# A two-layer diffusion step: the attention gate's modulation moved to VectorE, the output projection reordered, four weight buffers instead of five

## The chip, the cores and the metric

The kernel runs on one core of one Trainium2 chip. The core has five engines that run side by side and wait for each other through semaphores: TensorE (matmuls), VectorE, ScalarE, GpSimd, and SyncE, which here only issues transfers. The metric is device time in microseconds of one launch. The profile calls the engines PE (PEld is its loading of stationary operands), DVE, ACT, POOL and SP.

## The reference

One inference step of a two-layer network over 128 context tokens and 256 latent tokens, with 1024 features. Layer 0 mixes tokens by attention, layer 1 by a gated MLP; both are followed by a gated feed-forward network with a width-3 convolution. Six modulation vectors per layer come from a conditioning vector, one for context and one for latent tokens.

```python
def adaln(cond, w_ada, b_ada):
    mod = jax.nn.silu(cond) @ w_ada + b_ada
    return jnp.split(mod[:, None, :], 6, axis=-1)      # sm, cm, gm, sf, cf, gf

for l in range(2):
    sm, cm, gm, sf, cf, gf = adaln(c, w_ada[l], b_ada[l])
    h = rmsnorm(x, norm_mix_g[l]) * (1 + cm) + sm
    mix = attention(h) @ w_attn_out if l == 0 else chunk_gmlp(h, ...)
    x = x + gm * mix
    h = rmsnorm(x, norm_ffn_g[l]) * (1 + cf) + sf
    x = x + gf * conv_ffn(h, ...)
```

`w_ada` is 1024 x 6144 for each layer. In attention each latent token attends to 4 rows of 16 neighbours of its 4 x 64 grid with a learned bias, and to 128 cached context keys in the same softmax; context tokens attend to each other. There are 16 heads of 64 features.

## The kernel before

Features lie on the partitions (8 blocks `k` of 128), the 384 tokens on the free axis. Every float32 matmul is done as three: each operand is split into a rounded high half (a cast on ScalarE, line 96 or 108) and the low remainder (a subtraction on VectorE, line 97 or 109), and `mac` (lines 103 to 105) multiplies high by high, high by low and low by high. Weights come in units of 512 KB (128 x 1024): a transfer into one of three staging buffers, the cast into a buffer of the pool `whp`, the subtraction into one of `wlp`. Both pools have five buffers.

The stages follow each other: values of attention, attention by pairs of heads, output projection, feed-forward 0, gated MLP, feed-forward 1, output. From the attention by pairs to the first output tiles the order on TensorE, ScalarE, VectorE and SyncE is the order of the program text, written out by hand (`tc.manual_schedule`). Elsewhere a list scheduler fixes each engine's order before the run, by program order and readiness by its own estimates; `load(src, 50)` gives a unit's two halves 50 places of precedence.

*Modulations.* A part of them is computed on TensorE (class `Ada`): a block of 512 KB (`adw`) holds 128 rows of `w_ada` times one of the six vectors, four matmuls with 32 columns of conditioning run on it (line 190; each shows as two records), and after eight blocks ScalarE copies the sums and TensorE transposes them (`flush`, line 206). Here this is done for the gate GM and for SF and CF of layer 0: 24 blocks, three in each of the eight rounds. The rest is computed on VectorE (class `AdaV`): a transposed block of 512 KB gives one of eight parts of one vector, by one multiply-and-sum reduction (line 248) for each of the two conditionings and a small add (line 250). It needs the conditioning broadcast to all partitions (`cs`, two tiles, activated on ScalarE at line 239), which is prepared after attention. Both classes take their `adw` from one pool of four buffers.

*Rounds.* Round `t` works on a pair of heads. Its queries and keys were made in the round before; it computes scores for two blocks of latent queries, exponentials (line 534), the normalization (lines 539 and 541), and the transposes of the pair before (line 549) with the copies `turned`; between them TensorE has the products of the next pair (`products`, 24 matmuls each) and the values of the pair before (line 566). `ready` casts the next unit and fetches another (line 448). `bias` and `queries` (line 483) stand behind the second `ready`. At a round's end come `ada.run(3)` and `ada.load(3)`, then the next round issues the cached keys (`kT`, one buffer, line 468) on the same queue.

*Output projection.* `output(m, ks)` adds the blocks `ks` of output tile `m` (24 matmuls when complete); `residual` adds the gated tile to `x`, squares it, and `early` writes the next stage's raw input `hhi`, `hlo` of block `m` (line 342). Four tiles are begun before the last pair's values are there, and finished one after another.

*Starts of stages.* `norm_first` lets the next stage start before its RMS norm is known: four units multiply the raw input, and their results are scaled afterwards (`late`). Meanwhile `modulated` (lines 326 to 330) overwrites `hhi` and `hlo` with the normalized input for the units that follow.

## Time and profile before

| | |
|---|---|
| median of 3 runs | 1021.97 us (1020.61 to 1024.64) |
| the profiled execution's own time | 1021.36 us |
| its span (first to last instruction) | 1019.6 us |
| mean granted TensorE clock | 0.993 |
| busy share PE / DVE / ACT / POOL | 98% / 76% / 47% / 1% |

The profile page gives busy times by engine, then the chain of work that ended last, then groups of instructions by line: engine, operation, `out<-in`, shapes, count, busy time, mean duration, and the idle time of the engine just before them with what ended it. A timeline row gives start, duration, engine, line and operation; in brackets stands the idle time before it and its releaser. A row by windows gives, for a stretch of time, the busy time of PE, PEld, DVE, ACT and POOL, then the granted clock, the busy share of the DMA engines and GB/s.

### The profile page before, as it was taken

What the parts mean: (1) busy time and instruction counts of PE and PEld (TensorE: products, weight loads), DVE (VectorE), ACT (ScalarE), POOL (GpSimd) and SP (SyncE); (2) the same over time, 40 slices, a digit from 0 to 9 for tenths busy, and PEclk for the clock granted to TensorE, in tenths of its full rate; (3) what the DMA queues carried; (4) which work ended last, traced back from release to release, by engine and by line L of the source; (5) the groups of instructions that cost most, each with busy time, mean ns of one, the idle gap of its engine ahead of it and who ended that gap; (6) DMA issues with size and microseconds to landing.
All of it is one profiled execution on the core that took longest, in us unless ns stands there. A gap on an engine that the chain in (4) does not pass through costs nothing.

```text
span 1019.6 us, 15979 instructions
## 1 busy us (share of the span) xinstructions
PE 998.2 (98%) x6030; PEld 948.6 (93%) x6030; DVE 775.7 (76%) x1588; ACT 480.6 (47%) x841; POOL 14.7 (1%) x29
## 2 busy tenths in 40 slices
PE   7999999999999999999999999999999999999996
PEld 6788888789999999999998889999999999999996
DVE  3546566577999888999979989888598777777652
ACT  3355556557655555433354434343485444443331
POOL 1000000000000000000000000000000000000000
PEclk8999999999999999999999999999999999999999
DMA  7874645633465545576737746566325434335521
GB/s 277 310 233 143 214 172 201 227 103 126 136 191 169 163 147 161 146 240 205 225 119 257 241 158 200 179 207 186 104 83 166 144 124 125 124 114 171 161 72 62
DMA packets 53932, 172.96 MB, mean 170 GB/s; under 512 B 6224, under 2 KB 12512, under 8 KB 53856
## 3 DMA queue, kind: packets, MB, share of 16 engines
q1 hardware_dynamic: 52992, 170.11, 51.9%
q0 software_dynamic: 432, 1.06, 0.3%
q8 instruction: 47, 0.77, 0.3%
q10 hardware_dynamic: 432, 0.79, 0.2%
q14 instruction: 29, 0.24, 0.1%
HBM read 169.31 MB, written 2.62 MB: 169 GB/s over the span
## 4 chain that ended last, share of the span: by engine, by line
PE 91%; DMA 3%; ACT 2%; DVE 1%; issue 1%; SPq 1%; POOL 0%; POOLq 0%; ACTq 0%
PE bank L103 28%; PE bank L105 28%; PE bank L104 28%; DMA kT<-in_ckT 2%; DMA adw<-in_w_ada 1%; PE bank L781 1%; PE bank L145 1%; PE bank L566 1%; PE bank L517 1%; PE bank L190 1%; PE bank L549 1%; PE bank L282 0%; ACT pr L534 0%; SPq L66 0%; PE bank L300 0%
## 5 line engine op out<-in xcount | busy, mean ns | idle before, releaser
L96 ACT CAST hi<-st 128x1024 fp32r<-128x1024 f32 (+1 forms) x192 | 197.7, 1031 | 302.3 <-PE bank L104 249.0
L105 PE MATMUL bank<-hhi,lo 128*128 128x384 f32 (+1 forms) x960 | 325.1, 339 | 0.2 <-DVE lo L109 0.2
L103 PE MATMUL bank<-hhi,hi 128*128 128x384 f32 (+1 forms) x960 | 325.0, 339 | 0.0
L104 PE MATMUL bank<-hlo,hi 128*128 128x384 f32 (+1 forms) x960 | 324.7, 338 | 0.0
L97 DVE TENSOR_TENSOR lo<-st,hi 128x1024 fp32r<-128x1024 f32 (+1 forms) x192 | 229.9, 1198 | 67.9 <-ACT hi L96 67.6
L105 PEld LDWEIGHTS bank<-hhi,lo 128*128 128x128 f32 x960 | 181.1, 189 | 0.5 <-DVE lo L109 0.5
L103 PEld LDWEIGHTS bank<-hhi,hi 128*128 128x128 f32 x960 | 181.1, 189 | 0.4 <-ACT kT L473 0.2
L104 PEld LDWEIGHTS bank<-hlo,hi 128*128 128x128 f32 x960 | 180.4, 188 | 0.1
L248 DVE CUSTOM_DVE_ANT_0 junk<-adw,cs 128x1024 bf16<-128x1024 f32 x112 | 136.5, 1219 | 1.0
L105 PE MATMUL bank<-ahi,lo 128*128 128x384 f32 x352 | 118.9, 338 | 0.0
L104 PE MATMUL bank<-alo,hi 128*128 128x384 f32 x352 | 118.9, 338 | 0.0
L103 PE MATMUL bank<-ahi,hi 128*128 128x384 f32 x352 | 118.7, 338 | 0.0
L104 PEld LDWEIGHTS bank<-alo,hi 128*128 128x128 f32 x352 | 66.1, 188 | 0.0
L105 PEld LDWEIGHTS bank<-ahi,lo 128*128 128x128 f32 x352 | 66.1, 188 | 0.0
L103 PEld LDWEIGHTS bank<-ahi,hi 128*128 128x128 f32 x352 | 66.1, 188 | 0.0
L103 PE MATMUL bank<-hi,hhi 128*128 128x512 f32 x144 | 57.6, 404 | 1.8 <-ACT hhi L328 1.8
L104 PE MATMUL bank<-lo,hhi 128*128 128x512 f32 x144 | 57.4, 398 | 0.0
L105 PE MATMUL bank<-hi,hlo 128*128 128x512 f32 x144 | 57.3, 399 | 0.0
L374 DVE SCALAR_TENSOR_TENSOR x<-bank,mod,x 128x128 f32<-128x128 f32 x64 | 23.8, 412 | 35.9 <-PE bank L105 35.9
L103 PE MATMUL bank<-mhi,hi 128*128 128x384 f32 x128 | 43.3, 339 | 0.0
L105 PE MATMUL bank<-mhi,lo 128*128 128x384 f32 x128 | 43.2, 338 | 0.0
L104 PE MATMUL bank<-mlo,hi 128*128 128x384 f32 x128 | 43.1, 337 | 0.0
(154 smaller groups left out, 1268.4 us busy)
## 6 DMA issues: line engine op xcount, KB each, us to landing
st<-in_w_up SPq DMA_DIRECT2D x88, 512.0 KB, 3.6
adw<-in_w_adaT SPq DMA_DIRECT2D x56, 512.0 KB, 3.7
adw<-in_w_ada SPq DMA_DIRECT2D x40, 512.0 KB, 5.8
st<-in_w_down SPq DMA_DIRECT2D x32, 512.0 KB, 3.6
st<-in_w_qk SPq DMA_DIRECT2D x16, 512.0 KB, 3.6
st<-in_w_gu SPq DMA_DIRECT2D x16, 512.0 KB, 4.3
st<-in_w_gv SPq DMA_DIRECT2D x16, 512.0 KB, 4.5
st<-in_w_gout SPq DMA_DIRECT2D x16, 512.0 KB, 4.4
```

What stands on the lines that cost most here:

```text
L96: nc.scalar.copy(hi[:, :n], st[:, :n])
L97: nc.vector.tensor_tensor(lo[:, :n], st[:, :n], hi[:, :n].bitcast(F32), ALU.subtract)
L103: nc.tensor.matmul(out, a[0], b[0], start=start, stop=False)
L104: nc.tensor.matmul(out, a[0], b[1], start=False, stop=False)
L105: nc.tensor.matmul(out, a[1], b[0], start=False, stop=stop)
L145: nc.tensor.matmul(pa[32 * j:32 * j + 32, 0:P], cond_s[:, 4 * hf + kk, :], w[hf][:, kk, P * q:P * q + P], start=(kk == 0), stop=(kk == 3), ...
L190: nc.tensor.matmul(self.pa[32 * j:32 * j + 32, 0:256], cond_s[:, k, :], t[:, 256 * j:256 * j + 256], start=(k == 0), stop=(k == KD - 1), t ...
L248: tc.keep_in_program_order(nc.vector.tensor_tensor_reduce(self.junk, t, self.cs[c], 1.0, 0.0, ALU.mult, ALU.add, m[:, c:c + 1]))
L374: nc.vector.scalar_tensor_tensor(x[m][:, a:b], ps[:, a:b], mod(l, gate, m, c), x[m][:, a:b], ALU.mult, ALU.add)
L517: nc.tensor.matmul(sc[hh][:, cols], q[qp][HS[hh], qs:qs + P], k[kp][HS[hh], ks], start=i == 0, stop=i == 2)
L549: nc.tensor.transpose((ta[:, o:o + P] if g < 2 else tb[:, o - 512:o - 512 + P]), pr[:, b, g * P:g * P + P], ident)
L566: nc.tensor.matmul(pv[64 * hh:64 * hh + 64, cols], vv[:, P * t + 64 * hh:P * t + 64 * hh + 64], pT[hh][:, o:o + n], start=start, stop=stop ...
```

## The change

The gate GM of layer 0 leaves `Ada` and heads the list of `AdaV`. Of `AdaV.run`, loading a block and the two reductions become calls of their own (`load`, `half`), so that each round computes one block of the gate: one reduction behind each of its two normalizations. TensorE keeps SF and CF, 16 blocks: two before the first round and two in each of the first seven. `flush` no longer stands at the head of every block but after the queries. The broadcast conditioning is prepared before the rounds, in memory that comes from one buffer fewer in `whp` and in `wlp`.

In the last round there are no modulation matmuls; output tile 0 starts right behind the last scores, ahead of the transposes. Tiles 0 to 2 are begun early instead of 0 to 3, tile 2 lends its blocks 5 and 6 to stand behind the last values, and tiles 3 to 7 run whole, in banks of four pools, the residuals of tiles 0 to 4 three tiles behind. In `norm_first` the four units run one after another over blocks 0 to 6, and then each adds block 7; before, every block ran through all four units.

```diff
-    whp = ctx.enter_context(tc.tile_pool(name="whp", bufs=5))
-    wlp = ctx.enter_context(tc.tile_pool(name="wlp", bufs=5))
+    whp = ctx.enter_context(tc.tile_pool(name="whp", bufs=4))
+    wlp = ctx.enter_context(tc.tile_pool(name="wlp", bufs=4))
...
-            order = [(0, GM), (0, SF), (0, CF)]
+            order = [(0, SF), (0, CF)]
...
         def one(self, l, pc, k, t):
-            self.flush()
...
-            self.todo = (both(1, SM, CM)[:8]
+            self.todo = (one(0, GM) + both(1, SM, CM)[:8]
...
+        def load(self):
+            l, pc, k = self.todo.pop(0)
+            t = adp.tile([P, D], F32, name="adw", tag="adw")
+            nc.sync.dma_start(t, w_adaT[l, pc, k])
+            return l, pc, k, t
+
+        def half(self, c, l, pc, k, t):
+            m = mods[l][:, pc, k]
+            tc.keep_in_program_order(nc.vector.tensor_tensor_reduce(
+                self.junk, t, self.cs[c], 1.0, 0.0, ALU.mult, ALU.add, m[:, c:c + 1]))
+            if c:
+                nc.vector.tensor_scalar(m, m, b_ada[:, l, pc * 8 + k:pc * 8 + k + 1], None, ALU.add)
+                if pc in (CM, CF):
+                    gain(l, pc, slice(k, k + 1))
...
-        for k in range(KD):
+        for ks in (range(KD - 1), (KD - 1,)):
             for wi, p in zip(w, ps):
-                mac(p[:, :NT + 2], wsel(wi, k, slice(0, P)), h(k, slice(0, NT + 2)),
-                    k == 0, k == KD - 1)
+                for k in ks:
+                    mac(p[:, :NT + 2], wsel(wi, k, slice(0, P)), h(k, slice(0, NT + 2)),
+                        k == 0, k == KD - 1)
...
         nc.gpsimd.dma_start(sv_out, V[:, 0, :])
+        ada_v.start(csp)
...
-        ada.load(3)
+        ada.load(2)
+        block = ada_v.load()
...
         Q = queries(p)
+        ada.run(2)
+        ada.load(2)
...
             normalized(*e)
+            ada_v.half(0, *block)
...
-            if last:
-                ada.run(3)
-            else:
+            if not last:
                 K = keys(t + 1, kT, p)
             e = exps(1, sc, pr, pc)
+            if last:
+                break
...
             normalized(*e)
+            ada_v.half(1, *block)
+            p = products()
+            ready()
+            bias(btr)
+            Q = queries(p)
+            ada.flush()
+            if old is not None:
+                values(t - 1, pT)
+            ada.run(2)
+            block = ada_v.load()
+            ada.load(2)
...
         output(0, range(6), ps_mm)
+        pT.append(turned(1, turn(*old[1])))
+        normalized(*e)
         ready()
-        values(6, pT, ps_sc)
+        pv = bank(ps_sc)
         output(1, range(6), ps_sc)
+        values(6, pT, pv)
         ready()
+        ada_v.half(1, *block)
         pT = [turned(0, turn(pr[0], pc[0]))]
+        ada.flush()
         output(0, (6,))
         output(1, (6,))
         pT.append(turned(1, turn(pr[1], pc[1])))
-        output(2, range(7), ps_mm)
-        ready()
+        output(2, range(5), ps_mm)
         values(7, pT)
-        output(3, range(7), ps_sc)
-        ada.flush()
-        for m in range(4):
+        output(2, (5, 6))
+        for m in range(3):
             output(m, (7,))
-            residual(0, GM, m, out[m][1], (0, SF, CF))
-            if m == 1:
+        for m in range(3, KD):
+            output(m, range(KD), (ps_sc, ps_ta, ps_ad, ps_mm, ps_sc)[m - 3])
+            if m < KD - 1:
                 ready()
+            residual(0, GM, m - 3, out[m - 3][1], (0, SF, CF))
         order.__exit__(None, None, None)
-        for m in range(4, KD):
-            output(m, range(KD), ps_mm if m % 2 else ps_sc)
-            if m < KD - 2:
-                ready()
+        for m in range(KD - 3, KD):
             residual(0, GM, m, out[m][1], (0, SF, CF))
...
+    csp = ctx.enter_context(tc.tile_pool(name="cs", bufs=1))
     with tc.tile_pool(name="att", bufs=1) as pool, tc.tile_pool(name="attw", bufs=2) as wkp:
         attention(pool, wkp)
-    csp = ctx.enter_context(tc.tile_pool(name="cs", bufs=1))
-    ada_v.start(csp)
```

## The prediction, made before the changed kernel was seen

> **What bounds the kernel now.** I read the page first: the shares of busy time and the chain that ended last.

> ```profile
> span 1019.6 us, 15979 instructions
> PE 998.2 (98%) x6030; PEld 948.6 (93%) x6030; DVE 775.7 (76%) x1588; ACT 480.6 (47%) x841; POOL 14.7 (1%) x29
> PE 91%; DMA 3%; ACT 2%; DVE 1%; issue 1%; SPq 1%; POOL 0%; POOLq 0%; ACTq 0%
> L96 ACT CAST hi<-st 128x1024 fp32r<-128x1024 f32 (+1 forms) x192 | 197.7, 1031 | 302.3 <-PE bank L104 249.0
> ```

> TensorE is busy for 98% of the span, so outside the places where it waits only removed TensorE work can help, and every new wait costs its full length. The last row says that the casts of weights mostly sit idle until TensorE releases a buffer (249.0 us): they run as far ahead as the buffers let them. I then looked for the stretches in which something else leads, in the timeline of each engine. The first is the loop over the eight head pairs. Here is one round of it, rows picked from the timelines of VectorE, ScalarE, SyncE and TensorE (start, duration, line, tiles, in brackets the idle time before and what ended it), under the group of the six key issues of the full rounds.

> ```profile
> L468 SPq DMA_DIRECT2D kT<-in_ckT x6: 376/408/637, 87.6 to 166.8; - x6
> 119.24 0.42 SPq L468 DMA_DIRECT2D kT<-in_ckT  x1
> 124.27 0.48 DVE L541 TENSOR_SCALAR pc<-pc,st 128x128 f32<-128x128 f32 x2
> 125.20 1.22 DVE L109 TENSOR_TENSOR lo<-st,hi 128x1024 fp32r<-128x1024 f32 x1 [0.45 <-ACT hi L108]
> 127.00 0.62 ACT L108 CAST khi<-kT 128x512 fp32r<-128x512 f32 x1 [1.18 <-DMA kT<-in_ckT]
> 127.66 0.69 DVE L109 TENSOR_TENSOR klo<-kT,khi 128x512 fp32r<-128x512 f32 x1 [1.23 <-ACT khi L108]
> 130.38 0.75 DVE L541 TENSOR_SCALAR pr<-pr,st 128x384 f32<-128x384 f32 x2
> 131.98 1.22 DVE L109 TENSOR_TENSOR lo<-st,hi 128x1024 fp32r<-128x1024 f32 x1 [0.85 <-ACT hi L108]
> 132.63 1.50 PE L190 MATMUL bank<-adw,cond_s 128*32 128x256 f32 x24
> 133.23 0.33 SPq L448 DMA_DIRECT2D st<-in_w_qk  x1
> 133.66 1.33 SPq L176 DMA_DIRECT2D adw<-in_w_ada  x3
> 135.08 0.64 SPq L468 DMA_DIRECT2D kT<-in_ckT  x1
> ```

> The key issues run from 87.6 to 166.8, that is five intervals of 15.84 us, and this round has 135.08 - 119.24 = 15.84. It closes on itself without TensorE: the issue at 119.24 stands on SyncE behind four 512 KB loads, the cast of the keys waits for its landing until 127.00 (7.76 us), keys, exponentials, copies and the cast of the next unit take until 131.98, the second subtraction ("lo") ends at 133.20, its end frees the staging buffer for the fetch at 133.23, three modulation loads follow on the same queue, and then the next key issue. So in the rounds a us off TensorE gains nothing, and a us in this chain costs a us.

> **The added reductions.** Each round gets two VectorE reductions of 1219 ns, the second followed by an add of 221 ns:

> ```profile
> L248 DVE CUSTOM_DVE_ANT_0 junk<-adw,cs 128x1024 bf16<-128x1024 f32 x112 | 136.5, 1219 | 1.0
> L250 DVE TENSOR_SCALAR mod<-mod,b_ada 128x2 f32<-128x2 f32 x56 | 12.4, 221 | 0.4
> ```

> The first stands after 124.27 + 0.48 = 124.75. It fills the wait of 0.45 us, pushes the first "lo" by 0.8 us to 127.2, and the key subtraction at 127.66 still finds the engine free: nothing. The second stands after 130.38 + 0.75 = 131.13 and ends, with the add, near 132.5, where "lo" now starts at 131.98. Behind it wait the fetch, three modulation loads and the keys: 0.5 us in each of the six full rounds, 3.0 us. The queue itself keeps its length, one load for VectorE and two for TensorE instead of three.

> **The removed matmuls and the first round.** Three blocks are 24 records in 1.44 us (132.63 to the next matmul), so 0.48 us a block. In the rounds this is off the chain and counts nothing, likewise the transposes of the gate, now absent. The first round:

> ```profile
> 72.99 0.44 PE L517 MATMUL bank<-khi,qhi 64*128 64x384 f32 x2 [0.58 <-ACT qhi L482]
> 82.74 0.75 DVE L541 TENSOR_SCALAR pr<-pr,st 128x384 f32<-128x384 f32 x2
> 83.48 1.23 DVE L109 TENSOR_TENSOR lo<-st,hi 128x1024 fp32r<-128x1024 f32 x1
> 85.11 2.36 SPq L176 DMA_DIRECT2D adw<-in_w_ada  x3
> ```

> Two blocks (0.96 us) come ahead of the first scores, 0.58 of it in a wait. Their two reloads go out on SyncE ahead of the next keys, some 0.9 us of issue (1.33 / 3 x 2) and 1 MB of traffic; I take 0.8 us for both. Here "lo" follows the normalization at once (82.74 + 0.75 = 83.49), so the second reduction costs 1.3 us. The three loads took 2.36 us at 85.11 against 1.33 later; the earlier release of buffers should save half of that 1.0. So +1.6 us. Rounds together: 1.6 + 3.0 = **+4.5** (bounds 0, if VectorE's place is hidden, and 6).

> **The last round and the output projection.** This is where the change gains:

> ```profile
> 185.14 0.64 PE L190 MATMUL bank<-adw,cond_s 128*32 128x256 f32 x8 [0.77 <-DMA adw<-in_w_ada]
> 186.42 0.64 PE L190 MATMUL bank<-adw,cond_s 128*32 128x256 f32 x8 [0.64 <-DMA adw<-in_w_ada]
> 187.69 0.64 PE L190 MATMUL bank<-adw,cond_s 128*32 128x256 f32 x8 [0.63 <-DMA adw<-in_w_ada]
> 188.26 0.87 PE L549 MATMUL bank<-ident,pr 128*128 128x128 f32 x6
> 186.92 0.48 DVE L541 TENSOR_SCALAR pc<-pc,st 128x128 f32<-128x128 f32 x2
> 187.85 1.23 DVE L109 TENSOR_TENSOR lo<-st,hi 128x1024 fp32r<-128x1024 f32 x1 [0.45 <-ACT hi L108]
> 213.44 0.48 PE L103 MATMUL bank<-ohi,hi 128*128 128x384 f32 x1 [1.86 <-DVE x L374]
> 213.60:217.10 3.50, 3.50 (x12) 3.50 (x12) 2.79 (x7) 3.50 (x7) 0.00 (x0) 0.51 0.00 0
> ```

> The last three blocks wait for their loads one after another: from 185.14 - 0.77 to 188.26 is 3.9 us, all gone. The wait of 1.86 us for the residual that frees a bank goes too: the whole tiles get banks of pools that are idle by then, and a residual has a tile of matmuls beside it. Right behind this wait the granted clock fell.

> In the stretch from 213.60 to 217.10 the clock (the third number from the end) is 0.51, so 3.5 us did the work of 1.8: 1.7 us lost, which I take as gone with the wait. Against it stands 1.0 us: the first reduction of the last round comes between 186.92 + 0.48 and the "lo" at 187.85 and holds it until near 188.55, so it ends near 189.75, while TensorE, with no blocks to wait for, asks for this low half at 184.4 + 18 matmuls of output tile 0 (0.175 us each, from the two last rows of the next fence: 3.2) + the transposes (0.87) + 2 matmuls = 188.8. And 0.3 us for the moved transposes and the last split of the attention output, which now has two blocks of output tile 2 as its cover (6 matmuls, 1.06 us, against a cast and a subtraction of about that length); were that cover missing, it would be 1 us. Sum: -3.9 - 1.9 - 1.7 + 1.0 + 0.3 = **-6.2** (bounds -7.5 and -4).

> [...]

> **The starts of the next three stages.** Each begins with four weight units on the raw input, and only then is the input rewritten, scaled. The last of the three (the others have the same shape):

> ```profile
> 727.66 1.05 ACT L96 CAST hi<-st 128x1024 fp32r<-128x1024 f32 x1 [3.21 <-PE bank L104]
> 728.18 0.42 PE L103 MATMUL bank<-hhi,hi 128*128 128x386 f32 x1
> 728.74 1.23 DVE L97 TENSOR_TENSOR lo<-st,hi 128x1024 fp32r<-128x1024 f32 x1 [0.20 <-ACT hi L96]
> 734.14 1.01 DVE L326 SCALAR_TENSOR_TENSOR t<-x,mod,R 128x128 f32<-128x128 f32 x3 [1.60 <-ACT R L351]
> 736.79 1.00 DVE L326 SCALAR_TENSOR_TENSOR t<-x,mod,R 128x128 f32<-128x128 f32 x3
> 743.03 0.89 DVE L330 SCALAR_TENSOR_TENSOR hlo<-t,mod,hhi 128x128 fp32r<-128x128 f32 x2 [0.43 <-ACT hhi L328]
> 745.46 1.98 ACT L96 CAST hi<-st 128x1024 fp32r<-128x1024 f32 x2
> 746.65 0.34 PE L103 MATMUL bank<-hhi,hi 128*128 128x384 f32 x1
> 747.00 0.33 PE L105 MATMUL bank<-hhi,lo 128*128 128x384 f32 x1
> ```

> The four units take 746.65 - 728.18 = 18.5 us, and the fifth follows without a gap, for two reasons. Its cast (727.66) and its subtraction (728.74) are done before the stage begins, in the fifth buffer; and the rewriting starts at 734.14, because the old order reads block k of all four units before block k + 1, so that the first block is free after an eighth of the stage. It goes at 2.65 us for two blocks (734.14 to 736.79). The change takes both away. With four buffers the fifth unit's cast must wait until the first unit ends, which is where the casts at 745.46 stand; and with unit after unit the old first block is read last when the fourth unit begins: 22 of 32 groups of matmuls, 12.7 us, near 740.9. From there eight low halves and six scalings remain (two can be made ahead): 14 halves of 2.65 / 4, 9.3 us, so the last block is rewritten near 750.7, with 0.5 for the first cast. The fifth unit would use it at 746.65 + 21 matmuls = 750.3.

> Added to that is its own "lo" of 1.2 us, which formerly stood ahead of the stage. If VectorE takes it at once, the rewriting ends near 751.9 and TensorE loses 1.6 us; if it comes behind the rewriting, TensorE stands at its third matmul (747.0) until 751.9 and loses 4.9. A gain is excluded: no wait stands here now. The lower bound is 0, should the next unit's matmuls fill the hole. I take 3, between the two orders, because the engine's queue shows waits of only 0.43 us in which a "lo" can slip in. Three starts: **+9** (0 to 15, and 20 with a fall of the clock behind each stall).

> **Priced at nothing.** Two activations prepare the conditioning:

> ```profile
> L239 ACT ACTIVATE cs<-cs 128x1024 f32<-128x1024 f32 x2 | 2.0, 1050 | 0.0
> ```

> They move ahead of the rounds, where ScalarE (47%) has room; in front of the first casts they could cost their 2 us and a wait for their loads. In the steady parts one unit of run-ahead less (24 matmuls, 4.2 us) still leaves two whole units, some 8 us, since the casts wait for TensorE there (the page's row of 249.0 us); were VectorE late by more than that, its place in the row would turn into TensorE's wait.

> **The sum** stands against the profiled execution's own 1021.4 us (the median of the three runs is 1022.0): 1021.4 + 4.5 - 6.2 + 9 = 1028.7 us.

> **Rivals.** First, the new starts are covered: the order written out in advance fills the hole with the next unit's matmuls and slips the "lo" into the waits of VectorE. For it speaks that TensorE shows no gap there now; against it that VectorE has 9.3 us of work after 740.9 and TensorE 9.4 until 750.3, with the extra "lo" of 1.2 still to come. It decides by whether TensorE's first wait behind a start is under 0.5 us. Then 1028.7 - 9 = 1019.7, not slower. Second, TensorE bounds the rounds after all, and its blocks leave: 0.4 - 7 x 0.48 = -3.0 in place of +4.5, so 1021.2, and with the first rival also true 1012.2. Against it speaks the constant interval of 15.84. Third, the "lo" comes last at all three starts and the clock halves behind each: 14.7 + 5.1 instead of 9, so 1039.5. For it speaks that a wait of 1.86 us was enough for a fall. Fourth, the half clock near the end of attention belongs to no wait and stays: 1028.7 + 1.7 = 1030.4; the row of 0.51 right behind the wait speaks against it. [...]

> **How the numbers follow.** The forecast has 0.33 (its own range is 1024 to 1035), the half clock that stays 0.05, the starts covered 0.22, the rounds bound by TensorE 0.10, both of these 0.13, the serial starts 0.17. A measurement here can tell about 0.5%, 5.1 us, from no change: the marks are 1016.9 and 1027.1. Faster is nearly all the joint case, with a little of the covered one: 0.17. Same holds most of the covered case, the second rival alone and a fifth of the forecast: 0.36. Slower is the rest: 0.47. A range from 1014 to 1039 leaves most of the joint case below it and part of the serial one above.

> **What the profile would show.** Key issues 16.3 us apart instead of 15.84, with "lo" of a round's second half waiting for no cast but starting when VectorE is free; TensorE waiting about 1.5 us a round. No gap near 185 to 188 and none between the output tiles, and a clock of 1.0 where it fell. Behind the fourth unit of each start a wait of TensorE of 1.6 to 4.9 us for "lo" or for the rewritten input. I am wrong if those waits are absent, if the key interval does not grow, or if ScalarE stands in the first 20 us for the conditioning.

## The result and the profile after

The changed kernel takes 1040.13 us (median of four runs, 1038.53 to 1040.97) against 1022.67 us of the kernel before beside it: the measured ratio is 1.0181, 95% interval 1.0165 to 1.0197 (the two medians alone give 1.0171). It is 17.5 us slower. The prediction said 1028.7 us, with a range from 1014 to 1039: the sign was right, the size was not, and the range ended a microsecond too low. The profiled execution took 1040.97 us, its span is 1039.2 us. It was the slowest of the four, and its span is 19.6 us longer than that of the profile before (1019.6); the stretches below are taken from these two profiles and add up to that within 0.3 us.

The page of the changed kernel: span, busy time by engine, the chain that ended last, and the group of weight casts.

```profile
span 1039.2 us, 15876 instructions
PE 1001.4 (96%) x5964; PEld 947.1 (91%) x5964; DVE 796.2 (77%) x1627; ACT 480.2 (46%) x840; POOL 13.8 (1%) x29
PE 83%; DVE 8%; DMA 3%; ACT 3%; issue 2%; SPq 0%; POOL 0%; POOLq 0%; ACTq 0%; DVEq 0%
L96 ACT CAST hi<-st 128x1024 fp32r<-128x1024 f32 (+1 forms) x192 | 197.7, 1031 | 325.6 <-PE bank L104 251.3
```

TensorE shows 66 records fewer than before and yet was busy 3 us longer, with a lower granted clock (0.989 in the mean, 0.993 before). VectorE's share of the chain rose from 1% to 8%. Where it entered is in the page's groups, first before, then after: in the last field stands the idle time of TensorE ahead of the group, and what ended most of it.

```profile
L105 PE MATMUL bank<-hhi,lo 128*128 128x384 f32 (+1 forms) x960 | 325.1, 339 | 0.2 <-DVE lo L109 0.2
L103 PE MATMUL bank<-hi,hhi 128*128 128x512 f32 x144 | 57.6, 404 | 1.8 <-ACT hhi L328 1.8
```

```profile
L105 PE MATMUL bank<-hhi,lo 128*128 128x384 f32 (+1 forms) x960 | 326.8, 341 | 8.6 <-DVE lo L97 7.3
L103 PE MATMUL bank<-hi,hhi 128*128 128x512 f32 x144 | 58.3, 408 | 6.3 <-DVE lc L372 4.5
```

The matmuls that use a unit's low half (line 105) waited 0.2 us in all before and 8.6 after, and those of the gated MLP's second input wait for `lc`, the small copy with which VectorE finishes reading a PSUM bank.

To see where the time went I put marks into both timelines: the first scores, the first matmul of each start (386 columns), and TensorE's end. Differences between marks, in us:

| stretch | before | after | change |
|---|---|---|---|
| first scores to the eighth key issue | 93.84 | 94.46 | +0.6 |
| eighth key issue to the start of ffn0 | 65.08 | 60.05 | -5.0 |
| ffn0 with its start | 280.72 | 290.78 | +10.1 |
| gated MLP with its start | 215.55 | 223.73 | +8.2 |
| ffn1 with its start, to TensorE's end | 283.74 | 289.77 | +6.0 |

The attention as a whole became 4.4 us faster, where the prediction had 1.7. The three starts cost 24.3, where it had 9. The second row depends on the profile: the four other traces that keep the old end of attention have 67.2 to 69.4 us there, with half clock on two or three windows of 3.41 us instead of one, so the 5.0 are the least that any pair of these traces gives.

**The rounds.** One round of the changed kernel, rows picked from the timelines of SyncE, ScalarE and VectorE (with the first and last key issue of the six full rounds):

```profile
88.53 0.40 SPq L475 DMA_DIRECT2D kT<-in_ckT  x1
136.01 0.39 SPq L475 DMA_DIRECT2D kT<-in_ckT  x1
143.29 0.62 ACT L108 CAST khi<-kT 128x512 fp32r<-128x512 f32 x1 [1.23 <-DMA kT<-in_ckT]
146.67 0.75 DVE L548 TENSOR_SCALAR pr<-pr,st 128x384 f32<-128x384 f32 x2
147.33 1.22 DVE L246 CUSTOM_DVE_ANT_0 junk<-adw,cs 128x1024 bf16<-128x1024 f32 x1
148.73 1.22 DVE L109 TENSOR_TENSOR lo<-st,hi 128x1024 fp32r<-128x1024 f32 x1
150.40 0.38 SPq L241 DMA_DIRECT2D adw<-in_w_adaT  x1
151.83 0.39 SPq L475 DMA_DIRECT2D kT<-in_ckT  x1
167.18 0.39 SPq L475 DMA_DIRECT2D kT<-in_ckT  x1
```

The reduction stands where it was expected. From the normalization to "lo" it is 148.73 - 146.67 = 2.06 us, 1.60 before (131.98 - 130.38): the 0.46 us are there. But five intervals take 167.18 - 88.53 = 78.65 us, 15.73 each, where 16.3 was predicted and 15.84 stood before. Something else in the round became shorter. (Two traces of variants with the same rounds, in which the clock fell to half for 3.41 us near 90, have 16.0 us each; the others lie between 15.7 and 15.8.)

**The tail of attention.** Waits of TensorE in its timeline, and the stretch that ran at half clock before:

```profile
189.55 0.45 PE L105 MATMUL bank<-ohi,lo 128*128 128x384 f32 x1 [0.88 <-DVE lo L109]
196.69 0.44 PE L203 MATMUL bank<-ident,ada_sb 128*128 128x128 f32 x2 [1.48 <-ACT pT L564]
213.60:217.10 3.50, 3.50 (x22) 3.50 (x21) 2.47 (x6) 1.55 (x4) 0.00 (x0) 1.00 0.33 117
```

The waits for the last three blocks, the wait for the residual and the half clock are gone; the low half behind the first reduction costs 0.88 us (1.0 was predicted). New and unforeseen is a wait of 1.48 us for the bank in which the modulations are transposed: it is released by the copy `pT`, which stands on ScalarE behind a cast.

**The starts.** The start of ffn1, by windows: TensorE, its loads, VectorE, ScalarE and GpSimd busy, then clock and DMA. Before, then after:

```profile
728.18:746.65 18.47, 18.47 (x111) 18.29 (x110) 14.26 (x41) 8.98 (x21) 0.85 (x1) 1.00 0.11 39
734.28:740.28 6.00, 6.00 (x36) 6.00 (x35) 6.00 (x19) 3.36 (x8) 0.00 (x0) 1.00 0.00 1
```

```profile
741.74:760.22 18.48, 18.48 (x110) 18.31 (x110) 8.89 (x26) 6.37 (x15) 0.85 (x1) 1.00 0.12 40
747.80:753.80 6.00, 6.00 (x36) 6.00 (x35) 1.31 (x4) 0.00 (x0) 0.00 (x0) 1.00 0.01 3
```

TensorE does the same in the 18.5 us, VectorE 8.89 us of work instead of 14.26. In the second third it is nearly idle (1.31 us of 6.00; before, it was busy for all 6.00 there; the second row of each view): it cannot overwrite the input while the units are still reading it. The 5.4 us that it misses come out behind the start, in several places. The first three rows are from ffn1; the other three are from the gated MLP, where VectorE stood for 6.46 us and TensorE waited twice for `lc`:

```profile
761.19 0.44 PE L105 MATMUL bank<-hhi,lo 128*128 128x384 f32 x1 [0.45 <-DVE lo L97]
766.48 0.62 PE L103 MATMUL bank<-hhi,hi 128*128 128x384 f32 x2 [0.98 <-ACT hhi L333]
768.66 0.45 PE L105 MATMUL bank<-hhi,lo 128*128 128x384 f32 x1 [1.03 <-DVE lo L97]
531.76 1.15 DVE L335 SCALAR_TENSOR_TENSOR hlo<-t,mod,hhi 128x128 fp32r<-128x128 f32 x3 [6.46 <-ACT hhi L333]
539.26 0.47 PE L103 MATMUL bank<-hi,hhi 128*128 128x512 f32 x1 [2.43 <-DVE lc L372]
541.76 0.77 PE L103 MATMUL bank<-hi,hhi 128*128 128x512 f32 x1 [2.04 <-DVE lc L372]
```

The gated MLP differs from the other two stages. Behind its start TensorE needs all three banks of the pool `ps_mm`, and two of them hold results of the start until VectorE has read them (`late`), which it does here among the rewriting.

In ffn0 the first three waits are like those of ffn1. Some units later a transfer was issued late, at 261.5, behind the end of the low half that frees its staging buffer (261.1), and landed at 267.9; the cast behind it (and all that stands behind the cast on ScalarE) came late, and TensorE stood for the low half.

```profile
247.11 0.44 PE L105 MATMUL bank<-hhi,lo 128*128 128x384 f32 x1 [0.45 <-DVE lo L97]
252.58 0.62 PE L103 MATMUL bank<-hhi,hi 128*128 128x384 f32 x2 [1.17 <-ACT hhi L333]
254.76 0.69 PE L105 MATMUL bank<-hhi,lo 128*128 128x384 f32 x1 [1.04 <-DVE lo L97]
268.00 1.05 ACT L96 CAST hi<-st 128x1024 fp32r<-128x1024 f32 x1 [3.19 <-DMA st<-in_w_up]
271.89 0.69 PE L105 MATMUL bank<-hhi,lo 128*128 128x384 f32 x1 [2.91 <-DVE lo L97]
```

Behind these waits the granted clock fell three times, twice in ffn0 and once in the gated MLP (third number from the end of each row, windows of the changed kernel):

```profile
250.90:254.30 3.40, 1.65 (x8) 0.97 (x7) 3.11 (x9) 3.28 (x7) 0.00 (x0) 1.00 0.00 0
254.30:257.70 3.40, 2.94 (x9) 2.94 (x10) 3.40 (x10) 3.06 (x5) 0.00 (x0) 0.50 0.45 154
268.00:271.40 3.40, 0.98 (x6) 0.67 (x4) 1.90 (x4) 3.12 (x5) 0.00 (x0) 1.00 0.00 0
271.40:274.80 3.40, 2.91 (x9) 2.91 (x10) 3.34 (x7) 0.51 (x1) 0.00 (x0) 0.50 0.46 153
537.60:541.00 3.40, 0.47 (x1) 0.19 (x1) 3.40 (x12) 3.38 (x7) 0.00 (x0) 1.00 0.00 0
541.00:547.80 6.80, 5.76 (x13) 4.22 (x14) 6.04 (x13) 5.34 (x12) 0.00 (x0) 0.50 0.30 108
```

The clock of 0.50 for 3.4 + 3.4 + 6.8 = 13.6 us is, by an estimate from these rows, up to 6.8 us lost. Behind the start of ffn1 there is no such stretch.

### The profile page after: what moved, and what is told of

Its sections match the earlier page's. It is cut to its first block, busy times and chain, and to the rows that moved or that the text cites. A ratio compares the mean times of both kernels' runs of the same rounds, so it can differ in the third digit from the quotient of the medians.

```text
span 1039.2 us, 15876 instructions
## 1 busy us (share of the span) xinstructions
PE 1001.4 (96%) x5964; PEld 947.1 (91%) x5964; DVE 796.2 (77%) x1627; ACT 480.2 (46%) x840; POOL 13.8 (1%) x29
## 3 DMA queue, kind: packets, MB, share of 16 engines
q0 software_dynamic: 432, 1.06, 0.3%
## 4 chain that ended last, share of the span: by engine, by line
PE 83%; DVE 8%; DMA 3%; ACT 3%; issue 2%; SPq 0%; POOL 0%; POOLq 0%; ACTq 0%; DVEq 0%
PE bank L105 26%; PE bank L104 26%; PE bank L103 26%; DMA kT<-in_ckT 2%; DVE hlo L335 1%; DVE t L331 1%; DMA st<-in_w_up 1%; PE bank L796 1%; PE bank L145 1%; DVE lo L97 1%; ACT pr L541 1%; PE bank L573 1%; DVE junk L246 1%; PE bank L524 1%; DVE lo L109 1%
## 5 line engine op out<-in xcount | busy, mean ns | idle before, releaser
L96 ACT CAST hi<-st 128x1024 fp32r<-128x1024 f32 (+1 forms) x192 | 197.7, 1031 | 325.6 <-PE bank L104 251.3
L105 PE MATMUL bank<-hhi,lo 128*128 128x384 f32 (+1 forms) x960 | 326.8, 341 | 8.6 <-DVE lo L97 7.3
L103 PE MATMUL bank<-hhi,hi 128*128 128x384 f32 (+1 forms) x960 | 326.2, 340 | 2.6 <-ACT hhi L333 2.2
L104 PE MATMUL bank<-hlo,hi 128*128 128x384 f32 (+1 forms) x960 | 325.7, 340 | 0.0
L97 DVE TENSOR_TENSOR lo<-st,hi 128x1024 fp32r<-128x1024 f32 (+1 forms) x192 | 229.9, 1199 | 72.3 <-ACT hi L96 72.0
L105 PEld LDWEIGHTS bank<-hhi,lo 128*128 128x128 f32 x960 | 182.0, 190 | 12.1 <-DVE lo L97 9.2
L103 PEld LDWEIGHTS bank<-hhi,hi 128*128 128x128 f32 x960 | 181.7, 189 | 4.0 <-ACT hhi L333 2.8
L104 PEld LDWEIGHTS bank<-hlo,hi 128*128 128x128 f32 x960 | 181.5, 189 | 1.1 <-DVE hlo L335 0.9
L246 DVE CUSTOM_DVE_ANT_0 junk<-adw,cs 128x1024 bf16<-128x1024 f32 x128 | 156.1, 1220 | 1.3
L103 PE MATMUL bank<-ahi,hi 128*128 128x384 f32 x352 | 119.0, 338 | 0.2 <-issue 0.2
L104 PE MATMUL bank<-alo,hi 128*128 128x384 f32 x352 | 118.9, 338 | 0.0
L105 PE MATMUL bank<-ahi,lo 128*128 128x384 f32 x352 | 118.9, 338 | 0.0
L103 PEld LDWEIGHTS bank<-ahi,hi 128*128 128x128 f32 x352 | 66.1, 188 | 0.5 <-issue 0.5
L104 PEld LDWEIGHTS bank<-alo,hi 128*128 128x128 f32 x352 | 66.1, 188 | 0.0
L105 PEld LDWEIGHTS bank<-ahi,lo 128*128 128x128 f32 x352 | 66.1, 188 | 0.0
L103 PE MATMUL bank<-hi,hhi 128*128 128x512 f32 x144 | 58.3, 408 | 6.3 <-DVE lc L372 4.5
L104 PE MATMUL bank<-lo,hhi 128*128 128x512 f32 x144 | 58.7, 408 | 0.3 <-DVE lo L97 0.3
L105 PE MATMUL bank<-hi,hlo 128*128 128x512 f32 x144 | 58.5, 406 | 0.0
L380 DVE SCALAR_TENSOR_TENSOR x<-bank,mod,x 128x128 f32<-128x128 f32 (+1 forms) x64 | 23.9, 412 | 33.3 <-PE bank L105 33.3
L103 PE MATMUL bank<-mhi,hi 128*128 128x384 f32 x128 | 43.3, 339 | 0.0
L105 PE MATMUL bank<-mhi,lo 128*128 128x384 f32 x128 | 43.2, 337 | 0.0
L104 PE MATMUL bank<-mlo,hi 128*128 128x384 f32 x128 | 43.1, 337 | 0.0
```

The lines of the kernel that those rows point to most:

```text
L96: nc.scalar.copy(hi[:, :n], st[:, :n])
L97: nc.vector.tensor_tensor(lo[:, :n], st[:, :n], hi[:, :n].bitcast(F32), ALU.subtract)
L103: nc.tensor.matmul(out, a[0], b[0], start=start, stop=False)
L104: nc.tensor.matmul(out, a[0], b[1], start=False, stop=False)
L105: nc.tensor.matmul(out, a[1], b[0], start=False, stop=stop)
L246: tc.keep_in_program_order(nc.vector.tensor_tensor_reduce(self.junk, t, self.cs[c], 1.0, 0.0, ALU.mult, ALU.add, m[:, c:c + 1]))
```

## Experiments: the starts

Two theories for the 24 us: the order (O: the rewriting begins late because the last unit reads every block late) and the buffer (B: the fifth unit is cast only when the first of the four is finished). Four kernels fill the table of the two.

**a_old_4**, the changed kernel with the old order:

```diff
-        for ks in (range(KD - 1), (KD - 1,)):
+        for k in range(KD):
             for wi, p in zip(w, ps):
-                for k in ks:
-                    mac(...)
+                mac(...)
```

> The changed kernel with the old order of the stage starts (block after block over the four units), four weight buffers kept. The marks of the two traces put 24.1 us of loss into the three stage starts (10.0, 8.1, 6.0) and 4.7 us of gain ahead of them. Theory O (the unit-after-unit order does it: the rewriting of h can begin only when the last unit has passed each block, so banks, low parts of units and the clock suffer): most of the 24 us comes back, about 1020 us (1017 to 1024). Theory B (the missing fifth buffer does it: the fifth unit is cast only when the first unit of the four is finished, and everything behind it is late): little comes back, about 1036 us (1032 to 1041). Both theories half and half: about 1028 us.

**a_new_5**, the changed kernel with a fifth buffer after the attention:

```diff
+    rot = {"n": 0, "extra": None}
+    def weight_pools():
+        rot["n"] += 1
+        if rot["extra"] is not None and rot["n"] % 5 == 0:
+            return rot["extra"]
+        return whp, wlp
...
-        hi = whp.tile(...)
+        wh, wl = weight_pools()
+        hi = wh.tile(...)
...
+    whx = ctx.enter_context(tc.tile_pool(name="whx", bufs=1))
+    wlx = ctx.enter_context(tc.tile_pool(name="wlx", bufs=1))
+    rot.update(n=0, extra=(whx, wlx))
     with tc.tile_pool(name="ffn0", bufs=1) as pool, ...
```

> The changed kernel with its new order of the stage starts, and a fifth weight buffer that is opened after the attention and takes every fifth unit from the first unit of ffn0 on. Theory O (order): little comes back, about 1036 us (1032 to 1041). Theory B (buffer): most of 24 us comes back, about 1020 us (1017 to 1024).

**a_old_5** has both edits:

> The changed kernel with the old order of the stage starts and the fifth buffer after the attention: only the rounds, the tail of the attention and the output order differ from the kernel before. If the whole loss is in the stage starts and attention gains 4.7 us as the marks say: 1022.7 - 4.7 = 1018 us (1016 to 1020), which would beat both kernels. If the gain of the attention is given back at the start of ffn0 by some other cause (late loads, clock), 1022 to 1024 us.

**b_new_4** is the kernel before with the new order, and from ffn0 on without the fifth buffer:

> The kernel before with the new order of the stage starts, and only four weight buffers from ffn0 on (five in the attention as before): the start terms alone. If they cost what the marks of the changed kernel show, 1022.7 + 24 = 1047 us (1044 to 1050). With the 9 us of the prediction: 1032 us. If part of the 24 us is a consequence of the new attention tail (units loaded late into ffn0), about 1040 us.

Measured: a_old_4 1022.21 us (0.9992 to 1.0018 of the kernel before), a_new_5 1030.20 (1.0062 to 1.0109; outside the ranges of both theories), a_old_5 1018.86 (0.9960 to 0.9995), b_new_4 1046.00 (1.0220 to 1.0264; the kernel before 1021.42 beside them).

| | five buffers | four buffers |
|---|---|---|
| block after block | 1018.86 | 1022.21 |
| unit after unit | 1030.20 | 1040.13 |

The starts alone carry the loss: undone, the rest of the change is 2.6 us faster than the kernel before; put into the kernel before, they cost it 24.6 us. (In the trace of b_new_4, 21.0 us of that stand in the three stages with their starts; 4.3 stand in the stretch ahead of ffn0, where the half clock of the old end of attention fell on three windows instead of one.) The order is the larger part (11.3 us with five buffers, 17.9 with four), the buffer the smaller (3.4 and 9.9), and together they cost 6.6 us more than the two alone. That is as much as the half clock takes, of which neither a_old_4 nor a_new_5 shows any behind a start; that these are the same 6.6 us was not tested by itself, and one kernel with half clock behind a start (a_six_4, below) has it in the gated MLP alone.

Why the order costs: theory V says that it is VectorE's lost time, the rewriting begun late. The rival U says that it is the units coming one by one, with their low halves and banks. Two doses of the order tell them apart, both on the changed kernel with its four buffers:

```diff
-        for ks in (range(KD - 1), (KD - 1,)):
+        for ks in [range(4)] + [(k,) for k in range(4, KD)]:     # a_half_4
+        for ks in [range(6)] + [(k,) for k in range(6, KD)]:     # a_six_4
```

> The changed kernel (four buffers), with the starts going unit after unit over the first four blocks only and block after block over the other four. Theory V (what the new order costs is VectorE's time: it can't begin the rewriting before the fourth unit has read the first block, 22 groups of matmuls after the start instead of 4; here it is 13 groups, 7.5 us, while VectorE is ready for it at about 6.0 us in any case): of the 17.9 us between the new order (1040.1) and the old one (1022.2) only 1.5 of 6.7 parts are left, 4 us, so 1026 us (1022 to 1029). Rival U (the units taken one after another are the cost, through the low parts and the banks of the late ones, not the moment of the rewriting): half of it stays, 1031 us or more (1030 to 1036).

> The changed kernel (four buffers), with the starts going unit after unit over the first six blocks. Theory V (VectorE's time): in the 18.5 us of a start VectorE does 14.25 us of work in the old order, 13.7 with four blocks unit after unit (1021.6 us), 8.9 with seven (1040.1). Here the first block is free 19 groups of matmuls after the start, near 10.9 us, and VectorE gets 4.3 us done before and at most 7.5 behind: 11.8, so 2.4 us short at each of three starts, against 5.3 in the new order, which costs 6.0 each: about 2.7 us each, 1030 us (1026 to 1032). Rival S (a step: only the last block left alone makes banks and low parts late, the moment of the rewriting does not count): 1022 us.

Measured: a_half_4 1021.55 us, a_six_4 1029.67 us. The start of ffn1 by windows, in the order a_old_4, a_half_4, a_six_4, a_new_5 (the third busy time is VectorE's):

```profile
728.01:746.47 18.46, 18.46 (x110) 18.22 (x110) 14.25 (x41) 8.98 (x21) 0.85 (x1) 1.00 0.10 36
```

```profile
726.70:745.20 18.50, 18.50 (x111) 18.27 (x110) 13.68 (x41) 9.04 (x21) 0.85 (x1) 1.00 0.14 41
```

```profile
735.11:753.57 18.46, 18.46 (x110) 18.28 (x110) 10.51 (x31) 7.10 (x17) 0.85 (x1) 1.00 0.12 41
```

```profile
732.53:751.02 18.49, 18.49 (x111) 18.32 (x111) 8.93 (x26) 6.39 (x15) 0.85 (x1) 1.00 0.12 41
```

With four buffers, VectorE's work inside the start and the time go together: 14.25 us and 1022.2, 13.68 and 1021.6, 10.51 and 1029.7, 8.89 and 1040.1. Half of the units' blocks in the new order cost nothing, which U forbids; six of eight cost 7.5 us, which a mere step at the last block forbids. So the order costs by the moment at which the rewriting can begin, as V has it. V's price of about 2.7 us for each of the three starts did not come, though. Against a_half_4 the stages of a_six_4 are 0.3 us (ffn0), 6.1 (gated MLP) and 1.3 (ffn1) longer: nearly all of it is one wait for a bank in the gated MLP, with half clock for 6.83 us from 533.6 on.

```profile
535.29 0.76 PE L103 MATMUL bank<-hi,hhi 128*128 128x512 f32 x1 [3.91 <-DVE lc L372]
```

So the total that V gave for a_six_4 (1030) was in part luck, and what a missing us of VectorE costs differs by stage. The estimate for a_half_4 was too dark (1026): it took 1.5 us of VectorE's time for lost, and only 0.6 were. The fifth buffer does not bring VectorE's time back (8.93 us in a_new_5); in its trace no wait behind a start is over 1.8 us and the clock stays at 1.0 there.

## Experiments: the rounds

Here the time agreed with neither the prediction (+4.5) nor its second rival (-3.0). All kernels of this section that begin with r or k stand on a_old_5 (1018.86 us).

**r_none** leaves `ada_v.half(1, *block)` out of the seven full rounds (and sets its place to zero once), **r_twice** has it twice there (the add then puts the bias in twice, so the gate has other values):

> The changed kernel with the old starts and five buffers after the attention (1018.9), without the second VectorE reduction and its add in the seven full rounds (that half of the gate's modulation is left out). If the second reduction stands in the chain of the keys at 0.5 us in six rounds and 1.3 us in the first, as the prediction had it: 1018.9 - 4.3 = 1014.6 us. If it is not on the path: 1018.9 (1018 to 1020).

> The same kernel (1018.9) with the second reduction and its add done twice in each of the seven full rounds (same values). If it stands in the chain of the keys: 1.4 us more in each of seven rounds, 1018.9 + 9.8 = 1028.7 us. If VectorE has room there: 1018.9 to 1021.

Measured: 1015.09 us (-3.8) and 1030.26 us (+11.4). The second reduction is in the chain, at about the price that the prediction gave it (4.3 of its 4.5; the 11.4 are a weaker witness, because in that trace the clock fell to half for 3.41 us in three places of the rounds). The rounds grew by only 0.6, so something else must have become about 3 us shorter. The group of the key casts shows what, before, then after (eight casts; the last field is the wait for the landing of the keys):

```profile
L108 ACT CAST khi<-kT 128x512 fp32r<-128x512 f32 x8 | 5.0, 621 | 9.6 <-DMA kT<-in_ckT 9.6
```

```profile
L108 ACT CAST khi<-kT 128x512 fp32r<-128x512 f32 x8 | 5.0, 622 | 5.3 <-DMA kT<-in_ckT 5.2
```

That is 4.3 us less waiting, though four loads of 512 KB still stand ahead of the keys. Is it the layout of VectorE's load?

```diff
# r_strided
-            nc.sync.dma_start(t, w_adaT[l, pc, k])
+            if (l, pc) == (0, GM):
+                nc.sync.dma_start(t, w_ada[k * P:(k + 1) * P, 0:D])
+            else:
+                nc.sync.dma_start(t, w_adaT[l, pc, k])
```

> The changed kernel with the old starts and five buffers after the attention (1018.9), with VectorE's eight blocks of the rounds loaded as strided rows of 4 KB, like TensorE's blocks, instead of from one closed stretch (same bytes, the gate's values are other ones). The wait for the landing of the keys is 4.3 us shorter in the changed kernel (9.6 to 5.3 us in the group of the key cast). Theory L (the layout of the load does it): 1018.9 + 4 = 1023 us, and the wait near 9 us again. Rival W (TensorE's and the queue's other work does it, the layout nothing): 1018.9 (1018 to 1020), wait near 5 us.

Measured: 1018.45 us, and 4.8 us in that group. Not the layout. In the single rounds the cast of the keys starts either about 6.2 us or 7.1 to 8.0 us after their issue. The transfers behind a key issue, of the round at 119.24 before (until 127.0, its cast), of the round at 119.43 after (until 127.5, its cast), and of the round at 151.83 after (until 157.8; its keys landed at 158.1):

```profile
q8 instruction: 1, 0.02, 0.8%
kT<-in_ckT SPq DMA_DIRECT2D x1, 64.0 KB, 7.7
```

```profile
q8 instruction: 1, 0.02, 0.8%
kT<-in_ckT SPq DMA_DIRECT2D x1, 64.0 KB, 8.0
```

```profile
kT<-in_ckT SPq DMA_DIRECT2D x1, 64.0 KB, 6.3
```

Queue 8 carries instructions, 47 transfers of 16 KB in a run, most of them 0.9 to 1.2 us long. In the third window there is none yet; one begins at 157.85, 0.3 us before these keys landed. In the kernel before one fell among the loads of each of the six full rounds (mostly 16 to 17 us apart, nearly in step with the rounds), and all six waited 7.1 us or more. In the changed kernel, with 16 records of TensorE and its loads fewer in a round, they came 17 to 20 us apart; the two rounds that have one 3 to 4 us behind the key issue waited 7.3 and 8.0 us, the other four 6.1 to 6.4. One of these four has a block 1.9 us ahead of the issue, which is where two late rounds of the kernel before have theirs (2.0 and 2.4 us ahead, 7.3 and 7.6 us), so this does not decide it. TensorE's 2 x 6030 records of matmuls and loads are 257 for each of the 47 transfers (2 x 5964 and 254 in the changed kernel), so I took these transfers for blocks of TensorE's instructions, an estimate from the counts of the two pages; in question here is the cost for the transfers beside it.

To test this, the kernel before got other warming matmuls at its very start, which shift the blocks against the rounds (`b_tiny34` and `b_tiny50` have 34 and 50 in place of the 18 of the control):

```diff
# b_tiny18
     for _ in range(18):
-        nc.tensor.matmul(warm[:, :P], ones, ones, start=True, stop=True)
+        nc.tensor.matmul(warm[:, :2], ones, ones[:, :2], start=True, stop=True)
```

> A control on the kernel before: its 18 warming matmuls of 128 columns at the very start have 2 columns instead, so the number of TensorE's instructions is the same. Both theories: the key casts wait about 7.6 us after their issue in each round as before, time 1021.5 us, give or take 2 for the colder start.

> The kernel before with 34 such small matmuls at the very start in place of 18: 64 more instructions of TensorE ahead of everything, so that the blocks of 16 KB in which its instructions are loaded (one per round, 16 us apart in the kernel before) fall a quarter of a block earlier in the program. Theory I (the keys land late because a block of instructions, about 1 us on one DMA engine, falls among the loads ahead of them): the blocks come some 4 us earlier, at the fetch that stands 2 us ahead of the key issue or before it; some rounds escape: 1015 to 1021 us. Rival N (the block has nothing to do with it): 1021.5 us as the control.

> The kernel before with 50 such small matmuls, 128 more instructions, half a block. Theory I: the blocks fall 8 us earlier, between the landing of one round's keys and the next round's loads, so the waits of the key casts fall from 7.6 to about 6.2 us and seven rounds are up to 1.3 us shorter: about 1014 us (1012 to 1018), less a us of longer start. Rival N: 1021.5 to 1023 us.

Measured: 1022.69, 1031.28 and 1033.56 us. The small matmuls were not small: 18 of them took 7.84 us and 50 took 21.50, so the first scores moved from 73.02 to 81.04 and 86.25 us. Less that, the times are 1022.7, 1023.3 and 1020.3. The later start is a second change in these runs, and the subtraction takes it for harmless. The group of key casts in the control and in b_tiny50:

```profile
L108 ACT CAST khi<-kT 128x512 fp32r<-128x512 f32 x8 | 5.0, 622 | 9.8 <-DMA kT<-in_ckT 9.7
```

```profile
L108 ACT CAST khi<-kT 128x512 fp32r<-128x512 f32 x8 | 5.0, 623 | 3.0 <-DMA kT<-in_ckT 2.7
```

A quarter of a block did nothing for the time (the blocks moved to just ahead of the key issue, and five of six rounds still waited). Half a block took 6.8 us off the waits, which theory N does not explain, but only 2.4 us off the time, where theory I expected 1012 to 1018: other waits took the rest, the largest of them ScalarE's wait for the values on TensorE (line 566), 4.4 us over five key intervals instead of 0.4. So the runs speak for instruction blocks as a cause of late keys, without closing the case: that they account for the 3 us in the changed kernel stays open, and so do the rounds of these three traces that were late with the block ahead of the key issue or with none near it.

**k_early** issues the keys' load a round earlier, ahead of all those loads:

```diff
             if not last:
-                kT, btr = cache(t + 1), bias_load(t + 1)
+                if t == 0:
+                    kT = cache(1)
+                btr = bias_load(t + 1)
...
                 K = keys(t + 1, kT, p)
+                if t + 2 < NPAIR:
+                    kT = cache(t + 2)
```

> The same kernel (1018.9) with the load of a pair's cached keys issued one round earlier, right behind the previous pair's key split, so ahead of the unit fetch and the modulation loads on SyncE's queue. If the rounds close over the landing of the keys (issue, 6.9 us to landing, cast, exponentials, low part, fetch, loads, issue), the chain is cut: the interval falls from 15.9 us to what TensorE needs, about 15.0, in six rounds: 1018.9 - 5 = 1014 us. If something else closes the round at the same length: 1018.9 (1018 to 1020).

Measured: 1014.18 us (0.9919 to 0.9944 of the kernel before). Between the fourth and the eighth key issue TensorE now has no gap:

```profile
100.60:159.30 58.70, 58.70 (x445) 49.08 (x444) 47.60 (x122) 34.89 (x93) 2.15 (x4) 1.00 0.57 196
```

These four intervals take 14.7 us each, where the six full rounds took 15.7. The chain over the landing of the keys is what closed the rounds, as the prediction read it.

**k_early_t** also mends the last round, by moving the reductions and the transposes of the modulations behind what TensorE waits for; **k_early_th** has the starts of a_half_4 besides, with five buffers:

```diff
             normalized(*e)
-            ada_v.half(0, *block)
+            if not last:
+                ada_v.half(0, *block)
...
         ready()
-        ada_v.half(1, *block)
         pT = [turned(0, turn(pr[0], pc[0]))]
-        ada.flush()
         output(0, (6,))
         output(1, (6,))
+        ada.flush()
+        ada_v.half(0, *block)
+        ada_v.half(1, *block)
```

> The kernel with the early key loads (1014.2), and the last round of the attention altered: both VectorE reductions and the transposes of TensorE's modulations come behind the low parts that TensorE waits for (waits of 1.04 us for the low part behind the first reduction, and 1.64 us for the bank that the modulations' transposes use). If both waits go: 1014.2 - 2.7 = 1011.5 us. If the waits only move to the next low part: 1014.2 (1013.5 to 1014.5).

> The same kernel as the last, with the starts going unit after unit over the first four blocks, with five buffers. If VectorE's time is all that the order of a start moves, nothing changes against block after block: 1011.5 us (1010.5 to 1012.5), or the same as the other kernel if that misses. If taking units one by one helps late units: up to 1 us faster.

Measured: 1012.93 us (0.9901 to 0.9934) and 1012.46 us (0.9897 to 0.9930). By the medians 1.25 of the 2.7 us came. In the traces the stretch from the eighth key issue to ffn0 is 2.0 us shorter: the wait for the bank is gone, and that for the same low half is 0.29 us instead of 0.88. The starts in half the new order are worth as much as the old ones. Both kernels beat the one before by 8 to 9 us, and the changed one by 27.

## Why the prediction was wrong in size

- **The starts: +9 predicted, 24.3 measured.** This is the step that failed. The first half of its mechanism was right: rewriting held up until the fourth unit (predicted 12.7 us after a start and 0.5 for the first cast, the first low half at 531.76 - 518.01 = 13.75), the fifth unit's low half among the rewriting. But the wait of 1.6 to 4.9 us that it put behind the fourth unit was 0.45 in ffn0 and in ffn1, and the loss came later. Mis-sized was what followed. The prediction counted TensorE's first stall and stopped at the fifth unit; but VectorE was 5.4 us behind and could not catch up (in ffn1 it was busy for 28.3 of the 29.6 us behind the start), and the debt came back as low halves of later units, as banks that `late` frees (not mentioned at all), as a transfer fetched late, and as half clock. It also took the three starts to have one shape; the gated MLP needs three banks at once, and lost 8.2 us to two waits for them and the half clock behind.
- **"Priced at nothing": one unit less of run-ahead in the steady parts.** Nearly right with the old order, where four buffers cost 3.4 us, about 1.1 a stage. Behind the new starts the buffer was the cover, and its absence cost 9.9.
- **The rounds: +4.5 predicted, +0.6 measured.** The term that was worked out held: the second reduction costs 3.8 by its removal, and the first round took 1.2 of the 1.6. What was missing is a gain in the landing of the keys, which none of the rows that it read pointed to. This miss of 3.9 us hid a part of the miss in the starts, by luck. The observation named as a refutation, an interval that does not grow, came true, though the mechanism behind the term stood.
- **The tail: -6.2 predicted, -5.0 measured between the two profiles.** Four of five terms came as priced; the term of 0.3 us for the moved transposes should have been 1.5.
- **The half clock.** The prediction took the half clock near the end of attention as gone with the wait before it, against its fourth rival: it went with the wait (clock 1.00 from 213.60 to 217.10), and three new ones stand behind waits that begin with one of 1.17, 2.91 and 2.43 us. That this could double the price of a start stood in the range's upper bound (20), not in the sum.
- **The rivals.** The third (1039.5) has nearly the measured time, but not by its mechanism: the fifth unit's low half did not come last (245.84 in ffn0, with more of the rewriting behind it until 253), and the clock fell at two starts of three. The first rival's test, a first wait under 0.5 us, was met at ffn0 and at ffn1 (0.45 each), and the stages lost 10.1 and 6.0 us all the same: the first wait was the wrong thing to look at.

## What to carry to other kernels

When an edit makes a well-used engine wait, price the work that it misses there, not the first stall: VectorE's busy time inside the start of ffn1 (about 14, 10.5, 8.9 us) ranked the variants with four buffers, while TensorE's busy time in it was the same in each. It ranked them and did not price them: a missing us cost little in one stage and several in another. A buffer or a wait priced at nothing under one order has to be priced again under the other: here the two edits cost 11.3 and 3.4 us alone, and 21.3 together. And where a loop closes over one small transfer behind large ones, try to issue it a round earlier: here that was worth 4.7 us (1018.86 to 1014.18).

## What the runs showed of the hardware

Another thing is the 16 KB block on the instruction queue (47 in a run). In the three windows shown, a key transfer with a block beside it landed after 7.7 and 8.0 us, and one without after 6.3. In the b_tiny runs more instructions ahead moved the blocks against the rounds, and with 50 small matmuls in place of 18 the key casts waited 3.0 us in all instead of 9.8: a change of some matmuls at the start shifted waits in the rounds.
